# Hybrid encoder block on one core: the delta heads' masks move from GpSimd to VectorE and ScalarE

## The chip, the cores and the metric

The kernel runs on one core of a Trainium2 chip. The metric is the device time of one execution in microseconds (us), from runs of the whole program. The engines are TensorE (PE, with its weight loads PEld), VectorE (DVE), ScalarE (ACT), GpSimd (POOL) and SyncE (SP), which issues all the DMAs here.

## The reference

One layer over 1024 tokens of width 1024, in float32. The part that matters here is the gated DeltaNet of the mixer: 4 heads, two directions, chunked (in the kernel 128 tokens are worked on together, two chunks of 64 in the reference).

```python
proj = h @ w_in[l]                       # columns: attention q, k, v; delta q, k, v; gate; alpha; beta
conv = silu(conv5(qkv))                  # centred short convolution on the delta q, k and v columns
g    = -exp(a_log) * softplus(a + dt_bias)          # per token, direction and head
# _gated_delta_chunked, once per direction
g     = cumsum(g)                                    # inside a chunk
decay = exp(where(incl, g[i] - g[j], -inf))
lower = where(strict, einsum('id,jd->ij', k * beta, k) * decay, 0)
sol   = triangular_solve(lower + I, [v * beta, k * beta * exp(g)])
qk    = einsum('id,jd->ij', q, k) * decay
# then a scan over the chunks with a 128 x 128 state, o_fwd + o_bwd, norm, gate
```

Around it stand windowed attention, an output projection, cross-attention into 256 memory tokens and a SwiGLU feed-forward.

## The kernel before, in words

Large products run on TensorE in a rounded 32-bit format (`F32R`): each operand is split into a rounded high part and a low part, and three products (high x high, low x high, high x low) are summed. The high part is a copy on ScalarE (line 102), the low part a subtraction (`split`, line 103) on VectorE, or on the engine that the caller names. `load_w` (line 118 and on) fetches a weight block (`wraw`), splits it into `whi` and `wlo`, two buffers each, and is scheduled ahead of its use.

The mixer's first part is issued in a written order, `D0 P0 D1 P1 D2 P2 D3 P3 B0 B1`:

- `D h` (`delta_proj`) makes the three projections k, q, v of head h. Each is 48 products of 128x512 into two PSUM banks (L259), evicted by ScalarE (L281, L282), convolved by VectorE in four taps (`acc`, L284) and passed through Silu on ScalarE (L285). There are five `acc` buffers and three PSUM banks for these projections. The first k and q are projected earlier and do not go through `delta_proj`.
- `P h` (`prep`) works in two halves b of four 128-token blocks each, taken in turns. It forms `gm`, the decays G of four blocks times a triangular mask, for both directions (POOL, L459). It multiplies them by the opposite triangle on TensorE into one PSUM bank (L460), and takes the exponential E (ScalarE, L462). Then come transposes of k (L452), squares (L469) and their roots, the products k.k and q.k (L486) times E (`U`, `pc`; VectorE, L489 and L493), the masked copies `pm` of `pc` for both directions (POOL, L496; three buffers), and the scaled v (`kv`, L503). `U`, `kv` and `pm` are stored to DRAM. The `pm` stores of the last head are issued behind the loads of the second base inverse.
- `B g` (`base_inverse`) inverts the 32x32 diagonal blocks of a pair of heads: loads (`V`), two scalings (L527, L529), a chain of 30 pairs of small VectorE operations (L536, L538), a product on VectorE (L540) and one on POOL (L541).

The second part (`L0 L1 G0 G1 A4 V A0 A1 L2 L3 ...`) builds the larger inverses (`levels`), the attention and gate projections and the first attention windows; the third runs the scan over the chunks (`psc`) beside the memory's projections and the other windows. Output projection, cross-attention and feed-forward follow. The tile framework turns the written order into one queue for each engine, with a simulated timeline: work that is ready may be put ahead of work that waits, so projections of a later step fill TensorE during an earlier one. Each queue is then fixed, and runs in order.

Of the kernel before, what the change touches and what calls it, by code (L numbers as in the profile page):

```python
# [10 lines left out]
F32 = mybir.dt.float32  # L11
F32R = mybir.dt.float32r
I32 = mybir.dt.int32
AF = mybir.ActivationFunctionType
ALU = mybir.AluOpType
# [4 lines left out]
P = 128  # L20
# [3 lines left out]
NT = S // P  # L24
# [51 lines left out]
def tile_hybrid_block(  # L76
# [6 lines left out]
    nc = tc.nc  # L83
# [4 lines left out]
    if dump is None:  # L88
        def dump(name, ap):
            pass  # L90


    def f32(ap):
        return ap.bitcast(F32)

    def bc(ap, axis, shape):
        return ap.unsqueeze(axis).to_broadcast(list(shape))
# [10 lines left out]
    def pool(name, bufs, **kw):  # L108
        return tc.tile_pool(name=name, bufs=bufs, reuse_waits="tile", **kw)
# [8 lines left out]
    def load_w(src, k, n, eng=None, after=None):  # L118

        with tc.high_priority(AHEAD):  # L120
            raw = wp.tile([P, k, n], F32, tag="wraw", name="wraw")
            with ExitStack() as order_:
                if after:
                    order_.enter_context(tc.issue_after(after.ins))
                nc.sync.dma_start(raw, src.rearrange("(k p) n -> p k n", p=P))
            hi = wp.tile([P, k, n], F32R, tag="whi", name="whi")
            lo = wp.tile([P, k, n], F32R, tag="wlo", name="wlo")
            split(hi, lo, raw, eng=eng)
        return hi, lo
# [7 lines left out]
    sm = p12.enter_context(pool("sm", 1))  # L137
    C0, C1 = _AT["mUi"], _AT["mU"]
    C = sm.tile([P, C1 - C0], F32, name="C")
    mU_s = sm.tile([P, P], F32, name="mU_s")  # L140
    mL_s = sm.tile([P, P], F32, name="mL_s")
    prm = sm.tile([P, 24], F32, name="prm")
    nega = sm.tile([P, 8], F32, name="nega")
    p1 = ExitStack()
# [8 lines left out]
    cm = {n: (C[:, a - C0:a - C0 + P] if a < C1 else CE[:, a - C1:a - C1 + P]) for n, a in _AT.items() if n != "ident"}  # L153
# [40 lines left out]
    t1 = pa1.enter_context(pool("t1a", 2, side="right"))  # L194
# [14 lines left out]
    for hf in range(2):  # L209
        hi = hx.tile([P, KT, HALF], F32R, name=f"hhi{hf}")  # L210
        lo = hx.tile([P, KT, HALF], F32R, name=f"hlo{hf}")
        for j in range(4):
# [10 lines left out]
            for kq in range(2):  # L223
                pt = small()
                for k in range(4):
                    c = (4 * kq + k) * P
# [15 lines left out]
    nc.scalar.copy(cols, pt[:, :P])  # L242
    nc.sync.dma_start(CE, consts[:, C1:])
    nc.sync.dma_start(C, consts[:, C0:C1])
    nc.vector.tensor_copy(mU_s, cm["mU"])
    nc.vector.tensor_copy(mL_s, cm["mL"])

    nc.sync.dma_start(prm[:, 0:8], a_log[0].rearrange("d h -> (d h)").partition_broadcast(P))
    nc.sync.dma_start(prm[:, 8:16], dt_bias[0].rearrange("d h -> (d h)").partition_broadcast(P))
# [4 lines left out]
    def gemm_b(whi, wlo, act, psums, nk=KT):  # L254

        for ah, p_ in zip(act, psums):
            for k in range(nk):
                for i, (w, a) in enumerate(((whi, 0), (whi, 1), (wlo, 0))):
                    nc.tensor.matmul(p_, w[:, k, :], ah[a][:, k, :], start=(k == 0 and i == 0),  # L259
                                     stop=(k == nk - 1 and i == 2))  # L260

    def proj(src_cols, eng=None):
        whi, wlo = load_w(src_cols, KT, P, eng)
        pp = [pg.tile([P, 512], F32, tag="pg", name="pg") for _ in range(2)]
        gemm_b(whi, wlo, hT, pp)
        return pp
# [4 lines left out]
    t2 = pp_.enter_context(pool("t2", 2))  # L271


    def conv(pp, ci):
        cp = tcv.tile([P, S + 4], F32, tag="cp", name="cp", bufs=2)
        nc.gpsimd.memset(cp[:, 0:2], 0.0)
        nc.gpsimd.memset(cp[:, S + 2:S + 4], 0.0)
        acc = tcv.tile([P, S], F32, tag="acc", name="acc", bufs=5)
        taps = [cols[:, t * 12 + ci:t * 12 + ci + 1] for t in range(5)]
        for hf in range(2):  # L280
            nc.scalar.copy(cp[:, 2 + hf * HALF:2 + (hf + 1) * HALF], pp[hf])  # L281
            nc.scalar.activation(acc[:, hf * HALF:(hf + 1) * HALF], pp[hf], AF.Identity, scale=taps[2])  # L282
        for t in (0, 1, 3, 4):
            nc.vector.scalar_tensor_tensor(acc, cp[:, t:t + S], taps[t], acc, ALU.mult, ALU.add)  # L284
        nc.scalar.activation(acc, acc, AF.Silu)  # L285
        return acc

    def dcols(i, h):
        return w_in[:, 768 + (4 * i + h) * P:768 + (4 * i + h + 1) * P]
# [10 lines left out]
    t1 = pa1.enter_context(pool("t1b", 1, side="right"))  # L300
# [8 lines left out]
    for hf in range(2):  # L309
        pp = pg.tile([P, 512], F32, tag="pg", name="pg")  # L310
        for k in range(KT):
            for a in range(2):
                nc.tensor.matmul(pp, wabr[:, k, :], hT[hf][a][:, k, :], start=(k == 0 and a == 0),
                                 stop=(k == KT - 1 and a == 1))
# [27 lines left out]
    G = sm.tile([P, 2, 4, NT], F32, name="G")  # L342
# [6 lines left out]
    dump("G", G)  # L349
    dump("beta", beta)  # L350


    pt = small()
    pv = pt[:, 0:192].rearrange("p (s d n) -> p s d n", s=3, d=2)
# [85 lines left out]
    def prep(h, kc, qc, vc):  # L440

        g, hh = h // 2, h % 2
        for src, i in ((kc, 2), (qc, 3)):
            nc.sync.dma_start(d_kv[g][:, :, hh, i].rearrange("c p n -> p c n"), src.rearrange("p (c n) -> p c n", c=NT))
        def part(b):
            c4 = slice(4 * b, 4 * b + 4)

            def turned(src):
                p_ = small()
                for j in range(4):  # L450
                    o = (4 * b + j) * P
                    nc.tensor.transpose(p_[:, j * P:(j + 1) * P], src[:, o:o + P], ident)  # L452
                return p_.rearrange("p (c n) -> p c n", c=4)


            pa = small()
            for d, (mi, ml) in enumerate((("mUi", mL_s), ("mLi", mU_s))):
                gm = t2.tile([P, 4, P], F32, tag="gm", name="gm")
                nc.gpsimd.tensor_tensor(gm, bc(G[:, d, h, c4], 2, (P, 4, P)), bc(cm[mi], 1, (P, 4, P)), ALU.mult)  # L459
                nc.tensor.matmul(pa, ml, gm.rearrange("p c n -> p (c n)"), start=(d == 0), stop=(d == 1))  # L460
            E = t2.tile([P, 4, P], F32, tag="E", name="E")
            nc.scalar.activation(E, pa.rearrange("p (c n) -> p c n", c=4), AF.Exp)  # L462

            def squares(pk, rev):
                ss = t2.tile([P, 4], F32, tag="ss4", name="ss4", bufs=4)
                for j in range(4):
                    jk = t2.tile([P, P], F32, tag="jk", name="jk")
                    o = 3 - j if rev else j
                    nc.scalar.activation(jk, pk[:, j, :], AF.Square, accum_out=ss[:, o:o + 1])  # L469
                return ss  # L470

            kv = t2.tile([P, 4, 2, P], F32, tag="kv", name="kv")
            yield
            pk = turned(kc)
            nc.scalar.copy(kv[:, :, 0, :], pk)
            ss = squares(pk, False)
            nc.gpsimd.tensor_scalar(xk[:, h, c4], ss, EPS, None, ALU.add)
            nc.gpsimd.tensor_tensor(rootk[:, h, c4], xk[:, h, c4], phalf[:, 0:4], ALU.pow)
            if hh and b:
                beta_rows(g)  # L480
            for i, src in ((2, kc), (3, qc)):
                yield
                p_ = small().rearrange("p (c n) -> p c n", c=4)
                for j in range(4):
                    o = (4 * b + j) * P
                    nc.tensor.matmul(p_[:, j, :], kc[:, o:o + P], src[:, o:o + P], start=True, stop=True)  # L486
                if i == 2:
                    U = t2.tile([P, 4, P], F32, tag="U", name="U")
                    nc.vector.tensor_tensor(U, p_, E, ALU.mult)  # L489
                    nc.sync.dma_start(d_u[g][hh, c4].rearrange("c p n -> p c n"), U)  # L490
                else:
                    pc = t2.tile([P, 4, P], F32, tag="pc", name="pc")
                    nc.vector.tensor_tensor(pc, p_, E, ALU.mult)  # L493
                    for d, mi in enumerate(("mUi", "mLi")):
                        pm = t2.tile([P, 4, P], F32, tag="pm", name="pm", bufs=3)
                        nc.gpsimd.tensor_tensor(pm, pc, bc(cm[mi], 1, (P, 4, P)), ALU.mult)  # L496
                        unsaved.append((d_pz[g][d][c4, :, hh, 0].rearrange("c p n -> p c n"), pm))
            yield

            nc.gpsimd.tensor_scalar(epsq[:, g, :, 1 - b, hh], squares(turned(qc), b == 0), P * EPS, P * EPS * EPS,  # L500
                                    ALU.mult, ALU.add)
            yield
            nc.vector.tensor_tensor(kv[:, :, 1, :], turned(vc), bc(rootk[:, h, c4], 2, (P, 4, P)), ALU.mult)  # L503
            nc.sync.dma_start(d_kv[g][c4, :, hh, 0:2].rearrange("c p s n -> p c s n"), kv)
            if h < 3:
                save()

        together([part(b) for b in range(2)])

    def base_inverse(g):  # L510
# [195 lines left out]
    kqv = {0: kqv0}  # L706

    def delta_proj(h):
        kqv[h] = kqv.get(h, [])
        for i in (1, 0, 2)[len(kqv[h]):]:  # L710
            kqv[h].append(conv(proj(dcols(i, h), nc.gpsimd), 4 * i + h))


    def issue(order, table):
# [58 lines left out]
    pc = p2.enter_context(pool("pc", 5, space=PSUM))  # L773
# [395 lines left out]
    for k in range(HK):  # L1169
        p0, p1 = turned_k(xn, k), turned_k(xn, k + HK)  # L1170
        g0, g1 = gain("ffn", k), gain("ffn", k + HK)
        x12, t1, t2_, t3_ = (tr.tile([P, HALF], F32, name=f"r{i}", tag=f"r{i}") for i in range(4))
# [352 lines left out]
```

## Time and profile before

| | us |
|---|---|
| median of 3 runs | 1586.01 |
| lowest, highest | 1585.48, 1587.09 |
| the profiled execution | 1581.95 |
| its span, first to last instruction | 1580.1 |

In the rows of groups, "x16" is the count, then come the busy time in us and the mean of one in ns, and then the idle time of the engine just ahead of them, with what ended it. In timeline rows the first number is the start in us, the second the time in us; operations of one line that follow each other are merged ("x3"). The chain of work is followed back from the end of the stretch, from each step to what released it.

### The profile page before, as it was taken

The page shows a single profiled execution, that of the slowest core. Times are in us where ns is not written, and L with a number is a line of the kernel's source. Part 1 is how long each engine was busy: PE and PEld are TensorE (multiplying, and loading weights), DVE is VectorE, ACT ScalarE, POOL GpSimd, SP SyncE. Part 2 cuts the span into 40 slices and gives each one's busy share as a digit, 9 for nine tenths or more (in the row PEclk, how much of TensorE's full clock was granted, in tenths as well). Part 3 has the DMA queues.
Part 4 walks back from the last instruction along what each step waited for, and adds up shares of the span by engine and source line. Part 5 has one row for each costly group of instructions (what it writes and reads, how often), then busy time and mean ns, then how long its engine had stood idle before and what let it go on. Part 6 is the DMA issues. An engine that isn't in the chain of part 4 may idle for free.

```text
span 1580.1 us, 21010 instructions
## 1 busy us (share of the span) xinstructions
PE 1503.9 (95%) x7451; PEld 1256.4 (80%) x7451; DVE 1047.9 (66%) x1609; ACT 748.8 (47%) x1504; POOL 462.1 (29%) x432
## 2 busy tenths in 40 slices
PE   6999898999899989999999999999999999999998
PEld 5777777778799867788888777788888888888786
DVE  6855977965688865444346448777768654586665
ACT  6564452246866764564335566332232332444532
POOL 2364433232234500253301140433434433100021
PEclk9999999999999999999999999999999999999999
DMA  6244337473998585454222264443335333853354
GB/s 208 67 129 120 107 107 180 134 187 111 318 293 276 164 271 184 157 187 147 74 73 94 67 206 139 125 150 121 127 110 164 100 101 106 294 202 112 107 171 162
DMA packets 260485, 242.95 MB, mean 154 GB/s; under 512 B 33672, under 2 KB 199453, under 8 KB 260381
## 3 DMA queue, kind: packets, MB, share of 16 engines
q1 hardware_dynamic: 260381, 241.62, 48.6%
q8 instruction: 58, 0.95, 0.2%
q14 instruction: 46, 0.38, 0.1%
HBM read 172.07 MB, written 66.88 MB: 151 GB/s over the span
## 4 chain that ended last, share of the span: by engine, by line
PE 74%; DVE 11%; DMA 6%; ACT 4%; issue 2%; SPq 1%; POOL 1%; DVEq 0%; POOLq 0%; ACTq 0%
PE pmg L1021 10%; PE pD L1196 7%; PE pE L1196 7%; PE pg L259 7%; PE pA L1196 6%; PE pcq L259 6%; PE pdX L1386 5%; PE pdA L1386 4%; PE pB L1196 4%; PE psc L790 3%; DVE acc L284 3%; PE pdD L1386 2%; PE pcs L1102 1%; PE pco L1128 1%; PE pck L921 1%
## 5 line engine op out<-in xcount | busy, mean ns | idle before, releaser
L102 ACT CAST whi<-wraw 128x1024 fp32r<-128x1024 f32 x108 | 113.1, 1049 | 149.7 <-DMA wraw<-in_w_gate_up_dram 30.9
L103 POOL TENSOR_TENSOR wlo<-wraw,whi 128x1024 fp32r<-128x1024 f32 x48 | 117.9, 2456 | 191.1 <-ACT whi L102 168.6
L259 PE MATMUL pg<-hhi,whi 128*128 128x512 f32 x352 | 141.0, 401 | 0.0
L259 PE MATMUL pg<-hhi,wlo 128*128 128x512 f32 x352 | 140.8, 400 | 0.0
L259 PE MATMUL pg<-hlo,whi 128*128 128x512 f32 x352 | 140.3, 399 | 0.0
L103 DVE TENSOR_TENSOR wlo<-wraw,whi 128x1024 fp32r<-128x1024 f32 x60 | 74.4, 1243 | 76.8 <-ACT whi L102 72.6
L1021 PE MATMUL pmg<-whi,b 128*128 128x512 f32 x384 | 118.4, 395 | 2.7 <-ACT whi L102 2.2
L1196 PE MATMUL pA<-s,whi 128*128 128x512 f32 x352 | 109.6, 392 | 1.4 <-ACT m L1213 1.4
L284 DVE SCALAR_TENSOR_TENSOR acc<-cp,cols,acc 128x1024 f32<-128x1024 f32 x48 | 77.2, 1610 | 19.2 <-ACT acc L282 14.0
L1021 PEld LDWEIGHTS pmg<-whi,b 128*128 128x128 f32 x384 | 71.2, 188 | 17.9 <-ACT whi L102 2.7
L259 PEld LDWEIGHTS pg<-hhi,whi 128*128 128x128 f32 x352 | 67.2, 191 | 14.4 <-issue 0.7
L259 PEld LDWEIGHTS pg<-hlo,whi 128*128 128x128 f32 x352 | 67.1, 191 | 14.2 <-issue 1.0
L259 PEld LDWEIGHTS pg<-hhi,wlo 128*128 128x128 f32 x352 | 67.4, 191 | 13.6 <-issue 0.5
L1386 PE MATMUL pdX<-dhl,whi 128*128 128x512 f32 x264 | 76.1, 390 | 1.5 <-DVE zv L1441 0.8
L1196 PEld LDWEIGHTS pA<-s,whi 128*128 128x128 f32 x352 | 65.3, 188 | 15.2 <-ACT m L1213 2.0
L1273 POOL TENSOR_TENSOR act<-act,up 128x512 f32<-128x512 f32 x33 | 50.1, 1519 | 88.0 <-DVE up L1272 53.2
L1021 PE MATMUL pmg<-wlo,b 128*128 128x512 f32 x192 | 71.4, 392 | 0.0
L1196 PE MATMUL pA<-s,wlo 128*128 128x512 f32 x176 | 68.7, 391 | 1.1 <-DVE wlo L103 1.1
L102 ACT CAST whi<-araw 128x1024 fp32r<-128x1024 f32 (+1 forms) x36 | 35.4, 982 | 71.5 <-PE pdX L1386 27.6
L1416 POOL TENSOR_SCALAR frs<-sq 128x1 f32<-128x1 f32 x8 | 11.9, 1497 | 195.5 <-ACT jk L1405 194.6
L1245 POOL TENSOR_TENSOR sr<-wraw 128x512 f32<-128x512 f32 x22 | 29.9, 1359 | 128.5 <-DMA wraw<-in_w_gate_up_dram 128.4
L103 DVE TENSOR_TENSOR wlo<-araw,whi 128x1024 fp32r<-128x1024 f32 (+1 forms) x36 | 40.8, 1133 | 39.5 <-ACT whi L102 39.4
(408 smaller groups left out, 4158.9 us busy)
## 6 DMA issues: line engine op xcount, KB each, us to landing
wraw<-in_w_gate_up_dram SPq DMA_DIRECT2D x52, 512.0 KB, 3.9
kv<-d_kv SPq DMA_DIRECT2D x32, 512.0 KB, 7.3
wraw<-in_w_in_dram SPq DMA_DIRECT2D x22, 512.0 KB, 4.7
b<-in_w_down_dram SPq DMA_DIRECT2D x20, 512.0 KB, 6.8
araw<-d_as SPq DMA_DIRECT2D x20, 512.0 KB, 3.7
pz<-d_pz SPq DMA_DIRECT2D x32, 256.0 KB, 7.1
wraw<-in_w_ckv_dram SPq DMA_DIRECT2D x16, 512.0 KB, 7.6
wraw<-in_w_out_dram SPq DMA_DIRECT2D x16, 512.0 KB, 4.1
```

The source lines that it names most:

```text
L102: nc.scalar.copy(hi, src)
L103: (eng or nc.vector).tensor_tensor(lo, src, f32(hi), ALU.subtract)
L259: nc.tensor.matmul(p_, w[:, k, :], ah[a][:, k, :], start=(k == 0 and i == 0), stop=(k == nk - 1 and i == 2))
L284: nc.vector.scalar_tensor_tensor(acc, cp[:, t:t + S], taps[t], acc, ALU.mult, ALU.add)
L790: nc.tensor.matmul(out[:, d, h, :], lt[:, d, h, :], rt[:, d, h, :], start=True, stop=True)
L921: nc.tensor.matmul(pp, w[:, k, :], mT[a][:, k, :], start=(k == 0 and i == 0), stop=(k == KT - 1 and i == 2))
L1021: nc.tensor.matmul(pp[t], act[a][:, k, tt], w_[:, kk, :], start=(k == 0 and i == 0), stop=(k == KT - 1 and i == 2))
L1102: nc.tensor.matmul(pp[:, t2_, :], q[a][:, ct, tt], kr_[b_][:, ct, :], start=(j == 0 and i == 0), stop=(j == 1 and i == 2))
L1196: nc.tensor.matmul(out_, w[a][:, k, :], xx[b_][:, k, :], start=(start and k == 0 and i == 0), stop=(k == HK - 1 and i == 2), skip_group_ch ...
L1245: nc.gpsimd.tensor_tensor(s[0], b_[:, 0:HK], b_[:, HK:], ALU.add)
L1273: nc.gpsimd.tensor_tensor(o_, o_, up, ALU.mult)
L1386: nc.tensor.matmul(banks[t], a[:, k - k0, tt], w, start=(first and k == 0 and i == 0), stop=(k == NB - 1 and i == 2), skip_group_check=not ...
```

## The change

Four things, all in the delta heads:

- the masks `mU`, `mL` are kept as rounded copies (`mU_r`, `mL_r`); they hold only 0 and 1;
- G is split once into a rounded part `ghi` and the remainder `glo` (three small VectorE operations);
- `gm` is made by ScalarE: for each direction and each of the two parts, four scalings of the 128x128 mask by a column of `ghi` or `glo`, written in the rounded format; L460 then sums four rounded products in one bank, in place of two float32 products;
- `pm` and the low parts of the weights in `delta_proj` are made by VectorE.

```diff
-    mU_s = sm.tile([P, P], F32, name="mU_s")
-    mL_s = sm.tile([P, P], F32, name="mL_s")
+    mU_r = sm.tile([P, P], F32R, name="mU_r")
+    mL_r = sm.tile([P, P], F32R, name="mL_r")
...
+    ghi = sm.tile([P, 2, 4, NT], F32, name="ghi")
+    glo = sm.tile([P, 2, 4, NT], F32, name="glo")
+    ghr = t1.tile([P, 2, 4, NT], F32R, tag="ghr", name="ghr")
+    nc.vector.tensor_copy(ghr, G)
+    nc.vector.tensor_copy(ghi, f32(ghr))
+    nc.vector.tensor_tensor(glo, G, ghi, ALU.subtract)
...
-            for d, (mi, ml) in enumerate((("mUi", mL_s), ("mLi", mU_s))):
-                gm = t2.tile([P, 4, P], F32, tag="gm", name="gm")
-                nc.gpsimd.tensor_tensor(gm, bc(G[:, d, h, c4], 2, (P, 4, P)), bc(cm[mi], 1, (P, 4, P)), ALU.mult)
-                nc.tensor.matmul(pa, ml, gm.rearrange("p c n -> p (c n)"), start=(d == 0), stop=(d == 1))
+            n = 0
+            for d, (mi, ml) in enumerate((("mUi", mL_r), ("mLi", mU_r))):
+                for part in (ghi, glo):
+                    gm = t2.tile([P, 4, P], F32R, tag="gm", name="gm")
+                    for j in range(4):
+                        nc.scalar.activation(gm[:, j, :], cm[mi], AF.Identity, scale=part[:, d, h, 4 * b + j:4 * b + j + 1])
+                    nc.tensor.matmul(pa, ml, gm.rearrange("p c n -> p (c n)"), start=(n == 0), stop=(n == 3))
+                    n += 1
...
-                        nc.gpsimd.tensor_tensor(pm, pc, bc(cm[mi], 1, (P, 4, P)), ALU.mult)
+                        nc.vector.tensor_tensor(pm, pc, bc(cm[mi], 1, (P, 4, P)), ALU.mult)
...
-            kqv[h].append(conv(proj(dcols(i, h), nc.gpsimd), 4 * i + h))
+            kqv[h].append(conv(proj(dcols(i, h)), 4 * i + h))
```

More of the change, by code (lines that the diff above doesn't have):

```diff
@@ L244, in tile_hybrid_block @@
     nc.sync.dma_start(C, consts[:, C0:C1])
-    nc.vector.tensor_copy(mU_s, cm["mU"])
-    nc.vector.tensor_copy(mL_s, cm["mL"])
+    nc.vector.tensor_copy(mU_r, cm["mU"])
+    nc.vector.tensor_copy(mL_r, cm["mL"])
     nc.sync.dma_start(prm[:, 0:8], a_log[0].rearrange("d h -> (d h)").partition_broadcast(P))
```

## The prediction

> **What bounds the kernel now.** I read the page first, then busy time by stretches, then the chain of work cut to the stage that changes, then single operations.
>
> ```profile
> span 1580.1 us, 21010 instructions
> ...
> PE 1503.9 (95%) x7451; PEld 1256.4 (80%) x7451; DVE 1047.9 (66%) x1609; ACT 748.8 (47%) x1504; POOL 462.1 (29%) x432
> ...
> PE 74%; DVE 11%; DMA 6%; ACT 4%; issue 2%; SPq 1%; POOL 1%; DVEq 0%; POOLq 0%; ACTq 0%
> ```
>
> TensorE bounds the kernel as a whole, but that is an average. All four heads' delta work lies between 68 us (the decays G are ready) and 240 us; by stretch (columns: TensorE, its weight loads, VectorE, ScalarE, GpSimd, clock, DMA):
>
> ```profile
> 68.00:240.00 172.00, 160.60 (x782) 129.04 (x781) 119.71 (x137) 89.53 (x232) 81.69 (x82) 0.98 0.39 113
> 250.00:300.00 50.00, 43.66 (x220) 36.40 (x218) 48.12 (x93) 13.39 (x31) 17.21 (x12) 0.93 0.59 145
> 600.00:1580.00 980.00, 961.00 (x4395) 793.47 (x4393) 606.46 (x788) 407.62 (x689) 250.39 (x195) 1.00 0.42 138
> ```
>
> From 600 us on TensorE is full and nothing is edited. In the delta stage it idles 11 of 172 us, and right behind it VectorE is full (48.12 of 50) with the second base inverse, which cannot start before the fourth head's products are stored. So the edit is worth what it takes off the chain up to 240 us. That chain, cut to the stage, and its worst place:
>
> ```profile
> by line: DVE acc L284 22.8%; PE pg L259 19.3%; DVE tmpb L536 8.0%; DVE A L538 4.9%; issue 4.5%; PE ps L486 3.3%; PE ps L452 2.5%; DMA V<-d_u 2.3%; ACT L462 2.2%; ACT acc L285 1.8%; PE ps L460 1.8%; ACT whi L102 1.8%; DMA d_kv<-kv 1.7%; ACT
> ...
> 212.84 2.73 POOL A L541
> 215.57 1.99 POOL gm L459
> ...
> 217.61 2.08 PE ps L460 x2
> ```
>
> VectorE holds 22.8 + 8.0 + 4.9 = 35.7% of it (61 us), ScalarE some 6% in the lines shown. Twice GpSimd itself ends the wait: TensorE's decay product L460 stood behind gm, which stood behind the base inverse's POOL multiply.
>
> **The change part by part.**
>
> *The decay product on TensorE (L460).* Eight half-heads times two directions, recorded in two passes each: 32 records. Two timeline rows of the old form, then two of the rounded form, which has the same 128x512 shape:
>
> ```profile
> 206.05 1.02 PE L460 MATMUL ps<-gm,mL_s 128*128 128x512 f32 x2
> 206.91 1.02 PE L460 MATMUL ps<-gm,mU_s 128*128 128x512 f32 x2
> ...
> 208.00 0.40 PE L259 MATMUL pg<-hlo,whi 128*128 128x512 f32 x1
> 208.23 0.40 PE L259 MATMUL pg<-hhi,wlo 128*128 128x512 f32 x1
> ```
>
> Two passes take 0.86 us from start to start, 0.43 each; a rounded product 0.23. The new form has 8 x 2 directions x 2 parts = 32 products of one pass: 32 x 0.20 = 6.4 us off TensorE. L460 is only 1.8% of the chain (3.1 us, of which half goes, 1.5); but elsewhere TensorE is nearly full. Ends -1.5 and -6.4; I take -3.
>
> *gm off POOL (L459).* Waits, and what follows one:
>
> ```profile
> PE ps L460 <- POOL gm L459: 4.9, 2, 3.7
> POOL gm L459 <- PE ps L460: 4.1, 3, 3.1
> ...
> L460 PE MATMUL ps<-gm,mL_s x16: 590/591/1222, 71.1 to 218.6; 128*128 128x512 f32 x16
> ...
> 217.00:220.40 3.40, 2.79 (x6) 1.65 (x7) 3.37 (x2) 0.00 (x0) 2.54 (x2) 0.50 0.97 305
> ```
>
> TensorE lost 4.9 us in two waits. After the 3.7 us one the granted clock was 0.50 for 3.4 us and a product took 1222 ns instead of 591: another 1.7 us. The Trainium skill ("TensorE: Matmul & The Clock Gate", Part 1) says that an idle window of about 3.4 us halves the clock until TensorE has been busy for one window; the trace agrees with 0.50 after 3.7 us. Ends 0 (ScalarE makes it wait as long) and -6.6; ScalarE (fourth engine column: 0.00) is idle there, so I take -4.
>
> *The masks on ScalarE.* 4 heads x 2 halves x 2 directions x 2 parts x 4 chunks = 128 scalings of 128x128. The trace has the same operation wider (from SBUF, scale by a column):
>
> ```profile
> 353.30 1.71 ACT L663 ACTIVATE sc<-sc,es 128x256 f32<-128x256 f32 x4
> 364.38 2.14 ACT L663 ACTIVATE sc<-sc,es 128x384 f32<-128x384 f32 x4 [0.73 <-DVE es L661]
> ...
> L663 ACT ACTIVATE sc<-sc,es 128x256 f32<-128x256 f32 x16 | 6.8, 499 | 0.1
> L663 ACT ACTIVATE sc<-sc,es 128x384 f32<-128x384 f32 x48 | 25.7, 615 | 2.7 <-DVE es L661 2.7
> ```
>
> Start to start they take (1.71 - 0.50)/3 = 0.40 and (2.14 - 0.615)/3 = 0.51 us, 0.11 per 128 columns, so 0.29 at 128: 128 x 0.29 = 37 us, 9.3 per head. ScalarE has 172 - 89.5 = 82.5 us left. With some 6 to 8% of the chain on ScalarE this puts 2 to 3 us on it; ends 0 and +9.3 (the whole of the first head, whose masks cannot start before G). I take +3, the three small high/low operations on G (some 0.3 us each, by the row of G itself) among it.
>
> ```profile
> 67.45 0.29 DVE L344 TENSOR_TENSOR G<-la,nega 128x64 f32<-128x64 f32 x1
> ...
> 79.90 1.06 ACT L285 ACTIVATE acc<-acc 128x1024 f32<-128x1024 f32 x1
> ...
> 81.33 0.69 ACT L282 ACTIVATE acc<-pg,cols 128x512 f32<-128x512 f32 x1
> 82.04 1.28 ACT L462 ACT_TABLE_LOAD   x1
> ```
>
> No table load comes with them: L282 is the same function (Identity with a column as scale); it ran behind the Silu at L285 with no load of its own, and the next load belongs to the Exp at L462.
>
> The Trainium skill ("ScalarE: Activation LUTs", Rules for kernel authors) would put a plain multiplication on VectorE. By the rows here the 32 tiles would cost VectorE 32 x 0.65 = 21 us in place of ScalarE's 37, and the sum would be 21 x 0.36 - 3 = +4.5 us worse, because the chain here is VectorE's; so I do not follow it.
>
> *VectorE's contention goes.* VectorE beside POOL, and alone:
>
> ```profile
> L284 DVE SCALAR_TENSOR_TENSOR acc<-cp,cols,acc 128x1024 f32<-128x1024 f32 x41 | 68.4, 1667 | 19.2 <-ACT acc L282 14.0 <-POOL gm L459 4.4
> ...
> 113.90 8.65 DVE L284 SCALAR_TENSOR_TENSOR acc<-cp,cols,acc 128x1024 f32<-128x1024 f32 x4 [4.44 <-POOL gm L459]
> ...
> 113.78 2.41 POOL L103 TENSOR_TENSOR wlo<-wraw,whi 128x1024 fp32r<-128x1024 f32 x1
> 116.14 2.02 POOL L459 TENSOR_TENSOR gm<-G,C 128x512 f32<-128x512 f32 x1
> ...
> 192.99 1.27 DVE L284 SCALAR_TENSOR_TENSOR acc<-cp,cols,acc 128x1024 f32<-128x1024 f32 x1
> ```
>
> A convolution tap takes 1.27 us alone; the mean of 41 is 1.667, and four taps under wlo and gm took 8.65 instead of 5.1. That is 23% of the taps' time, 41 x 0.39 = 16 us, and of the 39 us on the chain 9. Ends 0 and -16; I take -9.
>
> *wlo and pm onto VectorE.* Ten low parts and sixteen masks:
>
> ```profile
> 212.58 1.23 DVE L103 TENSOR_TENSOR wlo<-wraw,whi 128x1024 fp32r<-128x1024 f32 x1
> 259.26 1.29 DVE L579 TENSOR_TENSOR D<-c,dmask 128x512 f32<-128x512 f32 x2
> ...
> L103 POOL TENSOR_TENSOR wlo<-wraw,whi 128x1024 fp32r<-128x1024 f32 x8 | 20.2, 2529 | 2.4 <-ACT whi L102 2.4
> L496 POOL TENSOR_TENSOR pm<-pc,C 128x512 f32<-128x512 f32 x16 | 23.9, 1512 | 21.3 <-DVE pc L493 11.7 <-DMA d_pz<-pm 9.4
> ```
>
> 10 x 1.23 + 16 x 0.65 (masking from SBUF, two in 1.29) = 22.7 us of VectorE. At the chain's VectorE share, 8 us; but wlo is fetched ahead and only a store reads pm, so I take +5 (ends 0 and +22.7). The stores' queue: the weight loads behind wlo come free earlier, 1.2 us instead of 2.5.
>
> *A wait that moves.* pm has three buffers, and the last mask of the last head waited 9.4 us for a store that is queued behind the base inverse's loads. On POOL nobody minded:
>
> ```profile
> 237.04 2.75 DMA d_u<-U
> ...
> 245.53 2.07 DVE L527 SCALAR_TENSOR_TENSOR A<-V,bB 64x1024 f32<-64x1024 f32 x1 [7.18 <-DMA V<-d_u]
> ...
> 247.81 2.19 POOL L496 TENSOR_TENSOR pm<-pc,C 128x512 f32<-128x512 f32 x1 [9.36 <-DMA d_pz<-pm]
> ```
>
> On VectorE the base inverse (L527) stands behind it if the mask comes first in the queue: 247.81 - 245.53 = 2.3 us at most, 0 if it is put behind. I take +1.
>
> *Sum:* -3 - 4 + 3 - 9 + 5 + 1 = -7 us on the chain up to 240 us. What follows hangs on that chain, so it moves along. The profiled execution took 1581.95 us (span 1580.1 and 1.85 around it), so 1575; the median of the runs, 1586.01, lies 4.1 above it, so I forecast 1579.
>
> **The rivals.**
>
> *The gain is larger:* all that went to VectorE and ScalarE finds gaps. TensorE's 6.4, the wait's 6.6 and 9 of contention, nothing added: -22 at most; with ScalarE's +3, -19: 1567. For it: VectorE is busy 119.7 of 172 us. Against it: the gaps lie between dependent steps, not where the new work is ready.
>
> *No change:* the added 22.7 us of VectorE weigh at the chain's share (+8, with +3 and +1), and only 9 of contention and 3 of TensorE go: 0, 1586.
>
> *Slower: ScalarE blocked in order.* gm has two buffers, and each half-head now fills four, so the third and fourth group of four scalings wait for TensorE to use the first two: 8 x 2 = 16 such waits. TensorE takes its work in order, and half a projection is 24 x 0.23 = 5.5 us. While ScalarE waits, the PSUM evictions that feed VectorE (L281, L282) stand behind. ScalarE would be busy 89.5 + 37 = 126.5 of 172, so it becomes the bound once a wait is 45/16 = 2.8 us; at 3.5 us the stage is 11 us longer, 1597. Against it: POOL, with the same two buffers, waited for TensorE three times for 4.1 us in all. For it: POOL needed no second pair within a half-head. The Trainium skill ("TensorE: Matmul & The Clock Gate", Architectural detail) calls ScalarE a strict FIFO, so the rule leaves no way around a waiting scaling; no run here shows that yet.
>
> That the change does not do what it says is no rival of weight: POOL keeps small powers and later masks, which stand on other lines.
>
> **How the numbers follow.** Likeliest, -4 to -13: 0.42, with 1579 and 1573 to 1582. Larger: 0.17, around 1567. No change: 0.18. Slower: 0.23, 1590 to 1604. A measurement tells 0.2% (3.2 us) from no change: faster is 0.42 + 0.17 less a little at the edge, 0.58; same 0.19; slower 0.23. From 1566 to 1596, half of the larger gain and about half of the slower case are left out.
>
> **What would show it.** Right: no gm, pm or wlo on POOL before 250 us; 32 L460 products 0.23 us apart; 128 scalings near 0.29 us; the mean tap down from 1.667 to about 1.3; the last d_u store some 7 us earlier than 237, and all later stages shifted by about as much. Wrong: ScalarE waiting for L460 for tens of us, taps waiting for ACT acc L282 longer than 14.0 us, VectorE waiting for the d_pz store, or a new order in the scan that gives the gain back.

## The result and the profile after

The changed kernel takes 1576.49 us (median of 4 runs, 1573.66 to 1577.59) against 1585.74 us of the first kernel beside it: ratio 0.9937, interval 0.992 to 0.9955, some 9 to 10 us faster. Its profiled execution took 1576.63 us, at the median. A second profile of the first kernel took 1585.88 us, at its median too, so the first one lay 4 us low by chance; the second is called "the first kernel, second profile" below and is the better partner for times late in the program.

The head of the page after:

```profile
span 1574.8 us, 21126 instructions
...
PE 1501.5 (95%) x7451; PEld 1257.4 (80%) x7451; DVE 1037.9 (66%) x1638; ACT 792.3 (50%) x1636; POOL 397.6 (25%) x390
```

ScalarE rose by 43.5 us, POOL fell by 64.5, VectorE by 10 although it received new work. The same stretches as before, of the kernel after (columns: TensorE, weight loads, VectorE, ScalarE, GpSimd, clock, DMA):

```profile
68.00:240.00 172.00, 167.72 (x852) 141.61 (x852) 115.76 (x165) 132.10 (x365) 19.76 (x43) 0.99 0.44 127
173.00:176.40 3.40, 3.38 (x9) 2.65 (x10) 3.40 (x6) 3.40 (x18) 0.19 (x1) 0.62 0.54 154
```

In the delta stage TensorE's idle time fell from 11 to 4.3 us of 172, and it fitted in 852 records instead of 782; VectorE has more room than before (115.76 against 119.71), and POOL is almost empty (81.69 to 19.76). The groups of the stage, 60 to 250 us:

```profile
L284 DVE SCALAR_TENSOR_TENSOR acc<-cp,cols,acc 128x1024 f32<-128x1024 f32 x40 | 52.3, 1308 | 0.7
L468 ACT ACTIVATE gm<-C,ghi 128x128 fp32r<-128x128 f32 x64 | 20.8, 400 | 2.9 <-PE ps L469 2.3 <-DVE ghi L356 0.5
L468 ACT ACTIVATE gm<-C,glo 128x128 fp32r<-128x128 f32 x64 | 20.4, 396 | 0.3 <-PE ps L469 0.3
L103 DVE TENSOR_TENSOR wlo<-wraw,whi 128x1024 fp32r<-128x1024 f32 x13 | 17.0, 1305 | 20.8 <-ACT whi L102 20.8
...
L506 DVE TENSOR_TENSOR pm<-pc,C 128x512 f32<-128x512 f32 x16 | 10.5, 689 | 3.3 <-DMA d_pz<-pm 3.1
...
L469 PE MATMUL ps<-gm,mU_r 128*128 128x512 f32 x16 | 6.4, 401 | 4.3 <-ACT gm L468 4.3
L469 PE MATMUL ps<-gm,mL_r 128*128 128x512 f32 x16 | 6.1, 413 | 0.0
```

The tap's mean is 1.308 us instead of 1.667, and the taps, which waited 19.2 us before, now wait 0.7. Last, the stores of U, which end the stage, after and in the first kernel's second profile (least, median and longest duration in ns, then the start of the first and of the last store in us):

```profile
L500 SPq DMA_DIRECT2D d_u<-U x8: 360/368/539, 87.3 to 230.3; - x8
```

```profile
L490 SPq DMA_DIRECT2D d_u<-U x8: 359/364/588, 82.1 to 237.6; - x8
```

The first head's store starts 5.2 us later, the last one 7.3 us earlier. From there the lead changes on its way: the scan's first load of the scaled v starts at 396.3 us instead of 401.3 (5.0 earlier), and the span ends 9.0 earlier (1583.8 to 1574.8).

### The profile page after: what moved, and what is told of

It is laid out like the page before. It is cut to its first block, busy times and chain, and to the rows that moved or that the text cites. A ratio compares the mean times of both kernels' runs of the same rounds, so it can differ in the third digit from the quotient of the medians.

```text
span 1574.8 us, 21126 instructions
## 1 busy us (share of the span) xinstructions
PE 1501.5 (95%) x7451; PEld 1257.4 (80%) x7451; DVE 1037.9 (66%) x1638; ACT 792.3 (50%) x1636; POOL 397.6 (25%) x390
## 5 line engine op out<-in xcount | busy, mean ns | idle before, releaser
L103 DVE TENSOR_TENSOR wlo<-wraw,whi 128x1024 fp32r<-128x1024 f32 x70 | 86.8, 1241 | 107.6 <-ACT whi L102 103.5
L103 POOL TENSOR_TENSOR wlo<-wraw,whi 128x1024 fp32r<-128x1024 f32 x38 | 92.3, 2430 | 163.9 <-ACT whi L102 152.6
L259 PEld LDWEIGHTS pg<-hhi,wlo 128*128 128x128 f32 x352 | 68.0, 193 | 13.5
L284 DVE SCALAR_TENSOR_TENSOR acc<-cp,cols,acc 128x1024 f32<-128x1024 f32 x48 | 62.5, 1304 | 0.7
```

Of the source, the lines that this page charges most:

```text
L103: (eng or nc.vector).tensor_tensor(lo, src, f32(hi), ALU.subtract)
```

## The experiments

Times in us against the first kernel are the ratio's distance from 1, times 1586; the ratio is to runs of the first kernel made beside the variant. The medians alone can differ from it by up to 2.5 us (masks on POOL below: 15 us faster by the ratio, 17.6 by the medians). Diffs are against the changed kernel unless said otherwise.

**The two halves.** One kernel has only the masked decays on ScalarE with the shorter product, one has only `pm` and the low parts on VectorE.

```diff
 gm_only
-                        nc.vector.tensor_tensor(pm, ...)
+                        nc.gpsimd.tensor_tensor(pm, ...)
-            kqv[h].append(conv(proj(dcols(i, h)), 4 * i + h))
+            kqv[h].append(conv(proj(dcols(i, h), nc.gpsimd), 4 * i + h))
 vec_only: the opposite choice at both places, and lines 456 to 460 as in the kernel before
```

> Only the decay masks change (ScalarE, rounded parts); pm and the weights' low parts stay on POOL. Theory A (the largest term is VectorE no longer standing behind POOL, and most of that stands behind gm: in the first kernel about 60% of the taps' extra time falls under a gm): -3 TensorE, -4 wait at the fourth head, +3 ScalarE, -5.5 taps = -9.5 us against the first kernel, mean tap about 1.45 us. Theory B (TensorE's shorter product and the lost wait make the gain, VectorE's relief and its new work cancel): -4 us. Rival C (ScalarE blocked in order): slower, as in the full change.

> Only pm and the ten low parts go to VectorE; gm stays on POOL in float32. Theory A: a third of the taps' relief (-3.5), the added VectorE work (+5), the moved wait (+1) = +2.5 us against the first kernel, mean tap about 1.5 us. Theory B: the relief is worth nothing on the chain, +6 us. If it comes out faster, the added VectorE work was over-priced.

> The first kernel against itself: ratio 1.000. Its earlier profile stood 4 us under the median of its runs; a second one should stand within 2 us of the median if that was chance.

The decays alone: 1.0015 [1.0004, 1.0026], 2.4 us slower. VectorE's work alone: 0.9984 [0.9973, 0.9994], 2.5 us faster. The first kernel against itself: 0.9992 [0.998, 1.0004]. Both theories missed for each half: the decays were expected at -9.5 or -4 us, VectorE's work at +2.5 or +6. So the halves sum to nothing, and together they bring 10 us: what the change is worth lies in the combination. The taps and their waits in the kernel with the decays alone:

```profile
L284 DVE SCALAR_TENSOR_TENSOR acc<-cp,cols,acc 128x1024 f32<-128x1024 f32 x41 | 62.8, 1532 | 34.4 <-ACT acc L282 33.6
```

and in the kernel with VectorE's work alone:

```profile
L284 DVE SCALAR_TENSOR_TENSOR acc<-cp,cols,acc 128x1024 f32<-128x1024 f32 x40 | 55.8, 1394 | 0.8
```

With the low parts still on POOL the taps wait 33.6 us for ScalarE's evictions; with them on VectorE the taps do not wait. Not all of that wait is gone, though: VectorE now stands at the low parts, which wait for their high parts (`whi`) from ScalarE, 20.8 us in the full change by its row above. The chain of the stage, 68 to 240 us, suggests why neither half is enough. Decays alone:

```profile
by line: DVE acc L284 20.5%; PE pg L259 16.1%; ACT gm L468 8.0%; issue 7.6%; DVE A L548 5.8%; DVE tmpb L546 3.9%; ACT whi L102 3.4%; ACT acc L285 3.1%; ACT jk L479 3.0%; ACT L472 3.0%; ACT acc L282 2.4%; DMA V<-d_u 2.1%; PE ps L496 2.1%; AC
```

VectorE's work alone:

```profile
by line: PE pg L259 34.9%; DVE acc L284 15.4%; issue 6.7%; PE ps L486 5.4%; DMA d_pz<-pm 4.2%; PE ps L452 3.8%; PE ps L460 3.1%; SPq L517 3.0%; DMA d_u<-U 2.9%; DVE tmpb L536 2.3%; DVE wlo L103 2.1%; DMA V<-d_u 2.1%; DVE A L538 2.0%; ACT L4
```

In the first the taps still lead (22.8% before, 20.5% now), and a shorter product on TensorE meets a chain that is VectorE's. In the second TensorE's projections lead (19.3% before, 34.9% now), and the long product stands among them (L460, 3.1%).

**The product without ScalarE.** If that reading is right it does not depend on who makes the masks. Two kernels make the 32 rounded masks on POOL, one operation each; one has the change's work on VectorE beside it, the other has not.

```diff
 gm_pool
-                    for j in range(4):
-                        nc.scalar.activation(gm[:, j, :], cm[mi], AF.Identity, scale=part[...])
+                    nc.gpsimd.tensor_tensor(gm, bc(part[:, d, h, c4], 2, (P, 4, P)), bc(cm[mi], 1, (P, 4, P)), ALU.mult)
 product_only: the same, with pm and the low parts on nc.gpsimd too
```

> The full change, but the 32 rounded masks are made by POOL in one operation each; pm and the low parts stay on VectorE. TensorE has the short product, ScalarE nothing more than in the first kernel, POOL 32 x 1.05 = 34 us. Theory A: VectorE stands behind POOL again, mean tap 1.5 us or more, within 3 us of the first kernel. Theory B: 3 to 6 us faster than the first kernel.

> The first kernel with only the product changed: POOL makes the masks in two rounded parts (32 operations of 128x512 in place of 16), TensorE sums four rounded products; pm and the low parts stay on POOL. Theory D (up to the output projection TensorE is the bound, so its 6.4 us count in full): 3 to 6.4 us faster than the first kernel. Theory A (VectorE standing behind POOL decides): POOL has 17 us more, so at least 3 us slower, mean tap above 1.67 us.

Together: 0.9905 [0.9889, 0.992], 15 us faster. The product alone: 0.999 [0.9979, 1.0001], no change. Neither came out as a theory had it (3 to 6 us faster or near the first kernel; 3 to 6.4 us faster or 3 us slower). With VectorE's work alone at -2.5 that is the same interaction as with the masks on ScalarE: the pair brings 11 us more than its halves' sum here, 10 us there. The chain of the product alone, 68 to 240 us, is still led by the taps:

```profile
by line: DVE acc L284 23.2%; PE pg L259 20.7%; issue 7.9%; DVE tmpb L545 7.8%; DVE A L547 6.0%; ACT whi L102 3.4%; PE ps L495 3.0%; PE ps L458 3.0%; DMA V<-d_u 2.9%; POOL gm L467 2.4%; ACT acc L282 2.1%; POOL A L550 1.6%; ACT cp L281 1.5%; 
```

The chain of the two together:

```profile
by line: PE pg L259 43.7%; DVE acc L284 11.2%; DVE A L547 6.8%; PE ps L495 6.2%; DVE tmpb L545 5.4%; PE ps L458 5.1%; issue 3.9%; DMA cz<-d_inv 2.6%; PE ps L468 2.2%; DMA V<-d_u 1.8%; POOL A L550 1.6%; POOL A L539 1.3%; DVE V L549 1.2%; DVE
```

and its taps:

```profile
L284 DVE SCALAR_TENSOR_TENSOR acc<-cp,cols,acc 128x1024 f32<-128x1024 f32 x40 | 59.9, 1496 | 0.8 <-POOL xk L486 0.2
```

This is a surprise for the contention: the taps are still at 1.496 us, less than half of the slowing is gone, and the kernel is nevertheless faster than the full change.

**The product in one part.** The full change, but 64 scalings in float32 and two float32 products, and so no split of G.

```diff
-                for part in (ghi, glo):
-                    gm = t2.tile([P, 4, P], F32R, ...)
+                gm = t2.tile([P, 4, P], F32, ...)       # scale=G[...], products with mL_s, mU_s
```

> The full change, but ScalarE makes the masks in float32 in one part: 64 scalings in place of 128, and two float32 products per half-head as in the first kernel. Theory A: TensorE's -3 goes, ScalarE's +3 halves: -4 + 1.5 - 9 + 5 + 1 = -5.5 us. Theory B: without the shorter product only the wait is left, -2.5 us. If ScalarE's scalings cost more than priced, it is faster than the full change.

0.9949 [0.9934, 0.9964], 8 us faster, where the theories had 5.5 and 2.5. The full change is 2 us better than this by the ratios, and the two intervals overlap, so that the rounded product gains anything over this version is not shown. The last U store here starts at 226.9 us, 3.4 earlier than in the full change; that would fit a price of the second 64 scalings in the stage, but one run does not tie a difference of this size to it.

**The masks on VectorE**, as 32 operations, and **three buffers** of `gm` in place of two, each alone and both together; then three buffers in the first kernel, and the full change with its two directions issued in the other order, which is the same work.

```diff
 gm_vector
-                    for j in range(4):
-                        nc.scalar.activation(gm[:, j, :], ...)
+                    nc.vector.tensor_tensor(gm, bc(part[:, d, h, c4], 2, (P, 4, P)), bc(cm[mi], 1, (P, 4, P)), ALU.mult)
 gm_bufs3
-                    gm = t2.tile([P, 4, P], F32R, tag="gm", name="gm")
+                    gm = t2.tile([P, 4, P], F32R, tag="gm", name="gm", bufs=3)
 gm_vector_bufs3: both.   before_bufs3: the kernel before with bufs=3
 after_turned
-            for d, (mi, ml) in enumerate((("mUi", mL_r), ("mLi", mU_r))):
+            for d, mi, ml in ((1, "mLi", mU_r), (0, "mUi", mL_r)):
```

> The full change, but the 32 rounded masks are made by VectorE in one operation each (128x512), none by ScalarE: VectorE +21 us, ScalarE -37. By the chain's shares of the prediction 4.5 us over the full change. By the rule of the Trainium skill (ScalarE: Activation LUTs, Rules for kernel authors: a plain multiplication belongs on VectorE) it is the faster one.

> The full change with three gm buffers in place of two. The rival of the prediction (ScalarE blocked in order behind TensorE) makes it at least 3 us faster than the full change. The traces show ScalarE's gm waiting 2.5 us in all, so I expect no difference beyond a new plan's 1 to 2 us.

> The masks by VectorE and three gm buffers. If the third buffer helped because ScalarE, in order, was held by a full pair, it does nothing here: 1567.8 within 2 us. If it helps whatever engine makes the masks (TensorE finds them earlier), 5 us or more faster, 1558 to 1563.

> The first kernel with three gm buffers: POOL's gm waited 4.1 us for TensorE, and only two masks are made per half-head. If the third buffer's gain hangs on four masks per half-head, no change (within 2 us). If it is a gain of its own, 5 us or more faster.

> The full change with the two directions of the masks made in the other order, otherwise the same work: what a new plan alone is worth. If plans differ by little, within 2 us of the full change (1574.5 to 1578.5). If the plan's luck is as large as the effects, 4 us or more to either side, and single variants' differences below that say nothing on their mechanism.

| kernel | median, us | ratio, interval | last U store | scan's first load |
|---|---|---|---|---|
| first kernel, second profile | 1585.69 | 0.9992 [0.998, 1.0004] | 237.6 | 401.3 |
| decays alone | 1588.67 | 1.0015 [1.0004, 1.0026] | 234.6 | 404.2 |
| product alone, masks on POOL | 1583.79 | 0.9990 [0.9979, 1.0001] | 240.6 | 403.9 |
| VectorE's work alone | 1583.70 | 0.9984 [0.9973, 0.9994] | 233.1 | 403.8 |
| full change | 1576.49 | 0.9937 [0.992, 0.9955] | 230.3 | 396.3 |
| its order turned | 1577.23 | 0.9952 [0.9938, 0.9965] | 229.8 | 395.9 |
| float32, one part | 1579.55 | 0.9949 [0.9934, 0.9964] | 226.9 | 396.8 |
| masks on VectorE | 1567.77 | 0.9888 [0.9876, 0.9901] | 223.6 | 388.3 |
| the same, three buffers | 1574.02 | 0.9929 [0.9915, 0.9943] | 221.5 | 388.3 |
| masks on POOL | 1568.46 | 0.9905 [0.9889, 0.992] | 229.6 | 391.7 |
| full change, three buffers | 1564.88 | 0.9881 [0.9861, 0.9901] | 226.2 | 390.4 |
| first kernel, three buffers | 1579.33 | 0.9964 [0.9952, 0.9977] | 226.0 | 397.2 |
| contention put back (below) | 1602.76 | 1.0115 [1.01, 1.0131] | 253.9 | 421.2 |

(The profiled execution of the full change with three buffers took 1574.31 us, the slowest of six; its median is over 9 us lower.)

Masks on VectorE are 8 us faster than the full change, and three buffers 9 us faster; these two have the lowest ratios of all, though the interval of the masks on POOL overlaps with both. But the masks on VectorE lose 6.5 us by the third buffer, although with three buffers they end the delta stage 2.1 us earlier than with two and start the scan at the same time: the loss comes between 400 and 530 us, where TensorE falls behind (2779 records up to 530 us against 2826). And the first kernel gains 6 us from a third buffer alone. So a third buffer's gain does not hang on four masks per half-head, nor on ScalarE. One thing goes with it in all three kernels: TensorE's wait for `gm`, which the third buffer takes from 4.9 us to nothing in the first kernel (6 us gained), from 4.3 to 0.8 in the full change (9 gained), and from 2.5 to 3.8 with the masks on VectorE (6.5 lost). The signs agree, the sizes do not, and everything else was planned anew as well; so the cause stays open.

Each edit can make a new plan of every queue. The turned order did not: in its trace all four engines run the operations of the full change in the same order, but for the exchanged directions. Its 1577.23 us, within the 2 us expected, shows how well a time repeats, and not what a plan is worth. The third buffer does change the order on every engine, but it also takes away waits, so what a plan alone is worth was not measured. As one buffer moves the time by 6 to 9 us either way, differences under some 6 us between single versions are not tied to a mechanism here.

How far TensorE has come by the end of the scan tells more than the end of the delta stage. Two stretches of the decays alone, then of the first kernel with three buffers (first engine column: TensorE's busy time and records):

```profile
0.00:240.00 240.00, 217.99 (x1077) 180.26 (x1078) 161.01 (x215) 172.01 (x430) 79.14 (x105) 0.99 0.44 128
0.00:530.00 530.00, 474.76 (x2704) 406.01 (x2705) 382.66 (x732) 336.44 (x834) 181.50 (x199) 0.97 0.59 174
```

```profile
0.00:240.00 240.00, 217.61 (x1041) 176.69 (x1042) 177.95 (x211) 123.30 (x292) 97.11 (x123) 0.98 0.45 130
0.00:530.00 530.00, 486.69 (x2775) 416.55 (x2776) 398.67 (x735) 287.98 (x702) 202.53 (x226) 0.97 0.61 176
```

At 240 us the first is 36 records ahead, at 530 us it is 71 behind, and its span is 8.8 us longer (1583.4 against 1574.6). Over all profiles the spans follow the records at 530 us almost in order (2568 records and 1600.6 us with contention put back, 2709 and 1583.8 in the second profile of the first kernel, 2760 and 1574.8 in the full change, 2826 and 1566.4 with the masks on VectorE), so much of what the versions differ by shows only behind the stage, where nothing was edited.

Masks on VectorE cost what the trace of before let expect (two groups of that kernel):

```profile
L467 DVE TENSOR_TENSOR gm<-glo,C 128x512 fp32r<-128x512 f32 x16 | 12.0, 749 | 0.0
...
L467 DVE TENSOR_TENSOR gm<-ghi,C 128x512 fp32r<-128x512 f32 x16 | 10.9, 682 | 7.7 <-PE ps L468 7.7
```

22.9 us of VectorE, which then is busy 137.31 of 172 us, and yet the stage ends 6.7 us earlier than in the full change. Its chain, 68 to 240 us:

```profile
by line: PE pg L259 31.6%; DVE acc L284 11.9%; issue 7.7%; DVE gm L467 3.7%; DMA d_pz<-pm 3.7%; PE ps L495 3.6%; DVE A L547 3.2%; DVE tmpb L545 3.2%; DMA V<-d_u 2.9%; DMA b<-d_beta 2.7%; DVE wlo L103 2.7%; PE ps L468 2.2%; PE ps L458 2.0%; 
```

TensorE's projections lead here, but VectorE still holds some 25% in the lines shown. That the added work is cheap because VectorE no longer leads is the likely reading, and not shown. The chain of the first kernel with three buffers, 68 to 240 us:

```profile
by line: PE pg L259 46.8%; DVE acc L284 10.4%; PE ps L486 7.3%; PE ps L452 5.6%; DVE A L538 4.9%; PE ps L460 4.0%; DVE tmpb L536 3.6%; DMA cz<-d_inv 2.3%; SPq L424 2.0%; DMA V<-d_u 1.8%; issue 1.6%; POOL wlo L103 1.4%; ACT whi L102 1.2%; DV
```

Here too the taps leave the chain (22.8% to 10.4%), and the stage ends 11.6 us earlier, with all the POOL work in place and the taps at 1.618 us. A stage that ends earlier does not need faster taps, nor taps that do not wait: they wait 18.5 us here.

**Contention put back.** The full change with 52 masks on POOL that nobody reads, on the evicted projections, on U and on pc.

```diff
+    def idle_mask(src, times):
+            nc.gpsimd.tensor_tensor(scr, src, bc(cm[...], 1, (P, 4, P)), ALU.mult)
+        if spare: idle_mask(cp[...], 2)      # and idle_mask(U, 2), idle_mask(pc, 2)
```

> The full change, and POOL gets 52 multiplications of 128x512 that nobody reads: two beside the taps of each convolution, two after each U and two after each pc (some 65 us of POOL, about what it lost). Theory A (what the change takes away is VectorE standing behind POOL): mean tap back from 1.31 to at least 1.6 us, the last U store 5 us later or more, and 5 to 10 us over the full change. Theory B (the shorter product and the lost wait): at most 2 us over the full change, since TensorE's queue has no POOL operation in it.

1.0115 [1.01, 1.0131], 18 us slower than the first kernel and 28 slower than the full change. Three groups of the stage:

```profile
L291 DVE SCALAR_TENSOR_TENSOR acc<-cp,cols,acc 128x1024 f32<-128x1024 f32 x40 | 61.2, 1531 | 0.7
...
L286 ACT COPY cp<-pg 128x512 f32<-128x512 f32 x20 | 11.8, 588 | 16.2 <-POOL scr L277 15.7 <-PE pg L259 0.4
L515 DVE TENSOR_TENSOR pm<-pc,C 128x512 f32<-128x512 f32 x12 | 11.6, 1008 | 2.3 <-DMA d_pz<-pm 2.2
```

The taps and the masks do slow down beside POOL (1.308 to 1.531, 0.689 to 1.008 us), the taps less than the 1.6 us expected, while the loss is far above the 5 to 10 us. It is not the slowing alone: the unread masks hold the buffers of the evicted projections, ScalarE waits 15.7 us for them, and TensorE 12.6 us for ScalarE's `gm`. The masks on POOL above have nearly the same taps (1.496) and are 33 us faster. So this run shows that the contention exists, not what it is worth.

## Why the prediction was right, and where not

The forecast was 1579 us, faster, and -7 us on the chain up to 240 us. The time is 2.5 us under it, and the last U store is 6.7 us earlier than in the profile it was made from (237.0 to 230.3). The direction of the mechanism holds: the taps left the chain. That the sum came out so close owes something to luck, since two of its terms failed (-4 and +5 below) and offset each other in part. The chain of the profiled execution after breaks off at 929 us; that of the same work in the turned order, 68 to 240 us:

```profile
by line: PE pg L259 63.2%; PE ps L496 6.8%; PE ps L458 4.6%; issue 4.4%; PE ps L469 3.7%; DMA V<-d_u 2.7%; DVE A L537 2.4%; DVE acc L284 2.1%; DMA d_u<-U 1.4%; SPq L527 1.4%; ACT gm L468 1.3%; ACT whi L102 1.2%; DVE pm L506 0.9%; DVE pc L50
```

Taps 2.1% instead of 22.8%, projections on TensorE 63.2% instead of 19.3%. By its steps:

- *The product, -3.* The 32 records of two passes became 32 of one, with means of 401 and 413 ns. What it is worth was not one number: about 0 while VectorE held the chain (product alone, 0.999), 12.5 us once VectorE did not (0.9905 against 0.9984, masks on POOL), 2 us, not clear of noise, where ScalarE pays for it with 64 more scalings (0.9937 against 0.9949). The -3 fits this last pair only. And the 12.5 us cannot all be the product: it takes 6.4 us off TensorE, and the two kernels lie 3.5 us apart at the last U store (233.1 and 229.6) and 12.1 at the scan (403.8 and 391.7).
- *gm off POOL, -4.* This term failed. TensorE waits for `gm` once, for 4.3 us, now for ScalarE, and the clock falls behind it as before (0.62 from 173.0 to 176.4 us):

```profile
PE ps L469 <- ACT gm L468: 4.3, 1, 4.3
...
ACT gm L468 <- PE ps L469: 2.5, 3, 1.4
```

  The bound "ScalarE makes it wait as long" came true: the maker of the mask changed, and the wait stayed. With three buffers it is 0.8 us.
- *The masks on ScalarE, +3.* The single scaling was sized rightly; the +3 on the chain no run isolates. Four scalings in one timeline row after:

```profile
75.76 1.28 ACT L468 ACTIVATE gm<-C,glo 128x128 fp32r<-128x128 f32 x4 [0.28 <-PE ps L469]
```

  (1.28 - 0.40)/3 = 0.293 us from start to start, forecast 0.29. A group of four takes 1.28, so 32 groups are 41 us rather than 37, and ScalarE's total rose by 42.6 in the stage. No table load comes with them, as forecast; but the new plan changes between Silu and Exp more often and has 17 loads of 1.283 us in the stage in place of 15. The first head's store came 5.2 us later, inside the +9.3.
- *Contention, -9.* The size of the effect was right (mean tap 1.308, forecast about 1.3). That it is what shortens the stage is not shown: two kernels end the stage early with taps at 1.496 and 1.618.
- *wlo and pm on VectorE, +5.* Durations as priced (pm 0.689, forecast 0.65; low parts 1.223 up to 240 us, forecast 1.23, with one later at 2.28 that lifts the mean to 1.305). Their price on the chain had the wrong sign: moving them alone came out 2.5 us faster, not slower, and with the shorter product they are worth 12 us (gm_only to the full change, 1.0015 to 0.9937) and 13.5 us (product alone to masks on POOL, 0.999 to 0.9905). Why is not shown: the taps' 19.2 us of waits went, but 20.8 us of waiting for ScalarE came at the low parts.
- *The moved wait, +1.* It was 0. The last mask waited 3.1 us in all, and the plan put it behind the base inverse's scalings:

```profile
240.99 2.06 DVE L537 SCALAR_TENSOR_TENSOR A<-V,bB 64x1024 f32<-64x1024 f32 x1 [7.05 <-issue]
243.08 1.22 DVE L539 SCALAR_TENSOR_TENSOR A<-V,b 64x1024 f32<-64x1024 f32 x1
244.33 0.69 DVE L506 TENSOR_TENSOR pm<-pc,C 128x512 f32<-128x512 f32 x1
```

- *"What follows moves along."* Not as a rule. Here 7.3 us at the U store became 5.0 at the scan and 9.0 at the end, by the second profile of the first kernel. In the two halves, stages that end 3.0 and 4.5 us earlier start the scan 2.9 and 2.5 us later. That the total came out near the forecast owes something to chance here too.
- *The rival of a blocked ScalarE* (16 waits, 2.8 us each to decide): ScalarE waited for TensorE's product three times, 2.5 us in all, far from a bound. The version with three buffers came out 9 us faster, where this rival had at least 3; but the first kernel, which has no mask on ScalarE, gained 6 as well, so that does not speak for it.
- *The choice against VectorE for the masks.* The Trainium skill ("ScalarE: Activation LUTs", Rules for kernel authors) would put the multiplication on VectorE; it was priced as 4.5 us worse. With two buffers the rule was right: 8 us better (0.9888 against 0.9937). With three it was not: 7.6 us worse (0.9929 against 0.9881). So these runs do not decide the choice. The price of +4.5 weighted VectorE's added 21 us by its share of the old chain (35.7%); by the lines shown above that share was some 25% with the masks on VectorE.

The terms for the product and for VectorE share one weak step: each was weighted by its engine's share of the chain before, and the chain passed to TensorE in the course of the change. Two bounds lie close together in this stage, VectorE's chain and TensorE's 161 of 172 us. An edit that relieves one alone leaves the other; the shares before cannot tell what the pair of edits gives. That these two bounds explain the interaction is a reading that the chains support and no run proves. Against it as the whole account stands the first kernel with three buffers: no work was taken off either engine, only TensorE's 4.9 us of waiting for `gm`, and still the taps leave the chain, the stage ends 11.6 us earlier and the kernel gains 6 us. The share that the luck of each plan has in it stays open, and so does the cause of the fast version with three buffers: its own gain of 9 us is more than the 3.5 us of wait that it removes. Its plan also has 13 table loads in the stage in place of 17; whether that counts was not tried.

## What to carry to other kernels

When a change relieves two engines, take the chain of the stage for each half alone before adding their gains: here the halves were worth +2.4 and -2.5 us and the pair -10. After the first half the shares of the chain are new, and a price that was worked out from the old shares may have the wrong sign. Where one scheduler plans all queues anew at each edit, run a version with an unrelated buffer more, and read from the traces whether the order of the queues changed: here the turned directions left it as it was, and the buffer did not. Differences below what such a version shows are not tied to a mechanism. And follow a lead beyond the edited stage, to where the bound engine has the same work left in both versions.

## What the runs showed of the hardware

VectorE slowed beside POOL only in some operations, and one place of the first kernel shows both kinds. First VectorE's timeline from 183 us (start, then time, in us):

```profile
182.69 0.41 DVE L536 TENSOR_TENSOR tmpb<-A 128x240 f32<-128x240 f32 x1
183.01 0.68 DVE L493 TENSOR_TENSOR pc<-ps,E 128x512 f32<-128x512 f32 x1
183.61 0.40 DVE L538 TENSOR_TENSOR A<-A,tmpb 128x240 f32<-128x240 f32 x1
183.93 0.68 DVE L493 TENSOR_TENSOR pc<-ps,E 128x512 f32<-128x512 f32 x1
184.53 0.90 DVE L536 TENSOR_TENSOR tmpb<-A 128x240 f32<-128x240 f32 x1
185.35 0.68 DVE L503 TENSOR_TENSOR kv<-ps,rootk 128x512 f32<-128x512 f32 x1
185.95 0.90 DVE L538 TENSOR_TENSOR A<-A,tmpb 128x240 f32<-128x240 f32 x1
```

and POOL's over the same time:

```profile
183.78 4.23 POOL L496 TENSOR_TENSOR pm<-pc,C 128x512 f32<-128x512 f32 x3 [1.98 <-DVE pc L493]
```

Before the mask starts on POOL, the base inverse's small operations take 0.41 and 0.40 us, under it 0.90. The products `pc` and the scaled v, each with one input in PSUM, take 0.68 us under it, as `pc` did at 183.01 ahead of it. The Trainium skill ("SBUF — State Buffer", Who interferes with whom) says that a VectorE operation with two inputs in SBUF contends with a GpSimd operation that reads SBUF, and one with at most one such input, outside the two-port performance modes, does not. These rows agree. So here it is the kind of operation beside POOL that decides, and a mean such as the taps' 1.667 us says nothing of the rest of VectorE's work.
